# First loads in the order of their use, and the first contraction tile by halves, in a two-layer encoder trunk

## The chip, the cores and the metric

The kernel runs on one core of a Trainium2 chip. A core has a matrix engine (TensorE, "PE" in the profile, with its weight loads "PEld"), a vector engine (DVE), a scalar engine (ACT), GpSimd (POOL) and a queue engine (SP) from which this kernel starts all its transfers. The metric is the device time of one execution in microseconds (us); lower is better.

## The reference

Two layers of a bidirectional encoder over 256 positions and 1024 channels, in fp32. What is computed, cut to what matters here:

```
for i in range(2):
    h = rms_norm(x, norm_mix_pre[i])
    z = h @ w_in[i]                     # latents and rotary key, window q/k/v, three gates
    o_a = latent attention, 8 heads     # from the latents c_q, c_kv, k_rope
    o_b = Re(2-D DFT of h), 4 channel groups
    o_c = windowed attention (|t-s| <= 128) with a distance term and a sink, 8 heads
    merged = sigmoid(g_a)*(o_a @ w_branch_a) + sigmoid(g_b)*(o_b @ w_branch_b) + sigmoid(g_c)*(o_c @ w_branch_c)
    x = x + rms_norm(merged @ w_out)
    x = x + rms_norm(SwiGLU(rms_norm(x)))
    x = x + rms_norm((p[i] @ w_ple_proj) * sigmoid(x @ w_ple_gate))
```

## The kernel before

The activations lie with channels on the 128 partitions and the 256 positions along the row: `x` is eight tiles of 128 x 256, in the buffer `gx` behind the gains (columns `C_ALL`). A product with a 128 x 128 weight tile is one matmul of 256 columns. For fp32 accuracy each operand is split into a high part (the value rounded to the matmul type, written by ACT) and a low part (the rest, written by DVE), and each product takes three matmuls: high by high, high weight by low activation, low weight by high activation.

**Weights.** 279 chunks of eight weight tiles (512 KB) come from memory in the order of their use. Class `Weights` handles a chunk c in two steps: `load` (L146) starts the transfer into one of three staging buffers `w`; `split` (L160) writes `wh` on ACT (L175) and `wl` on DVE (L180) into one of three pairs of buffers, and then calls `load` for the chunk three places on. Chunk 0 is loaded and split in two halves of 512 columns (`pieces`, L156), every later one in one piece.

**Order.** PE, ACT and DVE run their instructions in the order in which this Python code calls them. That order is made by a planner, class `Order`: it keeps a clock `now`, which each planned matmul moves on by `T_MM` (0.109), and for each of ACT, DVE, POOL and the transfers the time at which it will be free (`free`). All side work is generators that yield the time at which they want to go on; whenever PE's code lets the clock move, the due ones are resumed and their instructions fall in between. Times that the planner believes decide only the order; what then waits on the chip is decided by semaphores. Buffers matter too: `take("f2", ...)` hands out one of six scratch buffers of 2 KB a partition, and a generator that finds none free yields until one is (L252). Among the users of `f2` are the angle tables (`posr`, `di`, `df`, `ang`, `nturn`), the latents (`c01`, `c23`, `zk`), the window's value and query (`zvs`, `zq0`), the Fourier tables (`dft`) and the squares of a norm.

**Start.** The opening loads x in five transfers with chunks 0, 1 and 2 between them, then the constants `cs` (identity and selector matrix, L435). While nothing is there to multiply, `keep_warm` puts small bf16 matmuls into PE's order (`warm`, L414; `WARM[0]` is their spacing by the planner's clock). `first_x` (L649) splits the eight tiles of x, `pre_norm` sums their squares, and `rstd` turns the sum into a row factor: PE sums over partitions (`ss_`), DVE scales (`ms_`), POOL raises to the power -1/2 (`rt_`, L497), PE spreads it over the partitions with the identity (`pr_`, L503), ACT copies it out (`R_`).

The first product is `k_outer` (L371): four pairs of output tiles, `z1` 0 to 3 (latents, rotary and window key, window value and first query), are accumulated side by side over the contraction tiles k = 0 to 5 of x. One k uses one chunk: eight weight tiles, 24 matmuls, in three passes over the four pairs: high weight with high x, low weight with high x, high weight with low x. The last two k (`LATE`) follow pair by pair in `mains` (L334), which runs over up to eight weight tiles of a chunk with both parts of the activation (L357, L358) and then with the low weights (L364).

`tables` (L669) asks for positions, sink and distance mask from the planner's time 6.0 on, has POOL form the differences of positions at 16.0, and from `TAB` = 18.0 on makes, by some dozen small DVE instructions, the distance (`dist`) and the rotary angles (`ang`, `nturn`), whose sine (`KC`) ACT takes. After the first product `latents` (L802) scales the four latent tiles, `window_vq0` (L856) the value and the first query, whose value is turned by PE (`vct`); `fourier_tables` splits the DFT tables; then the string `MIX` orders the pieces of the window attention, Fourier, gates (`gp`) and branches.

Of the kernel before, what the change touches and what calls it, by code (L numbers as in the profile page):

```python
# [17 lines left out]
P = 128  # L18
# [11 lines left out]


T_MM = 0.109
T_SEM = 0.18
MIX = "CCGGCCPPGPPGGBGGGBGGGBBG"
TAB = 18.0
PACE = 5.6
LATER = 0.3
ONACT = 2
STAGE = 3
WARM = (0.33, 0.15)  # L40
URGENT = (4.5, 2.5)
LATE = (2, 2, 2)
CT = 8
# [92 lines left out]
class Weights:  # L136
# [9 lines left out]
    def load(self):  # L146
        c, O = len(self.staged), self.O
        if c >= NCHUNK:
            return
        w = self.stage.tile([P, CT * P], F32, tag="w", name=f"w{c}")  # L150
        for s in self.pieces(c):
            self.nc.sync.dma_start(out=w[:, s], in_=self.dram[c, :, s])
        O.free["dma"] = max(O.free["dma"], O.now) + 1.5
        self.staged.append((w, O.free["dma"] + (2.0 if c else 1.0)))

    def pieces(self, c):  # L156
        n = CT * P // (1 if c else 2)
        return [slice(k, k + n) for k in range(0, CT * P, n)]

    def split(self):  # L160
# [23 lines left out]
    def idle(self, engine, c, us):  # L184

        O = self.O
        while (self.quiet or O.free[engine] > O.now + 0.1) and (c * CT - len(self.order)) * 3 * T_MM > us:
            yield O.now + 0.3
# [33 lines left out]
def encoder(ctx: ExitStack, tc: tile.TileContext, order, gxT, pT, pos, cst, dftT, mask, sink, wts, outT):  # L222
    nc = tc.nc
# [19 lines left out]
    O = Order()  # L243
    rd = {}
# [68 lines left out]
    ws = Weights(nc, O, stage, high, wts, order)  # L313

    def mm3(ps, lhs, rhs, start, stop, skip=False):
# [3 lines left out]
        T.matmul(ps, ll, rh, start=False, stop=stop, skip_group_check=skip)  # L319
        O.spend(3 * T_MM)  # L320

# [12 lines left out]
    def mains(ps, keys, rhs, start=True, stop=True, skip=False, there=None):  # L334

        i = 0
        while i < len(keys):
# [17 lines left out]
            for j in group:  # L355
                rh, rl = rhs(j)
                T.matmul(ps, w[j][0], rh, start=start and j == 0, stop=False, skip_group_check=skip)  # L357
                T.matmul(ps, w[j][0], rl, start=False, stop=False, skip_group_check=skip)  # L358
                O.spend(2 * T_MM)
                step()  # L360
# [10 lines left out]
    def k_outer(pairs, key, rhs, done, late):  # L371


        for k in range(KT - late):
            have(("x", k))
            if k == 0:
                weights(2 * len(pairs))
                keep_warm(None)
            weights(2 * len(pairs))
            w = [[ws.get(key(k, n, c)) for c in range(2)] for n in range(len(pairs))]  # L380
            xh, xl = rhs(k)
            for part, mov in ((0, xh), (1, xh), (0, xl)):
                for n in range(len(pairs)):
                    for c in range(2):
                        T.matmul(pairs[n][:, c, :], w[n][c][part], mov, start=(k == 0 and c == 0 and part == 0 and mov is xh),  # L385
                                 stop=False, skip_group_check=True)
                        O.spend(T_MM)
                    if n % 3 == 2:
                        O.step()
            ws.flush()  # L390
        for n in range(len(pairs)):
            ks = range(KT - late, KT)
            for c in range(2):
                mains(pairs[n][:, c, :], [key(k, n, c) for k in ks], lambda q: rhs(ks[q]), start=False, skip=True,
                      there=lambda q: ("x", ks[q]))
            done(n)
# [26 lines left out]
    mhalf = one.tile([P, 4], F32, tag="mhalf", name="mhalf")  # L423
    G.memset(mhalf, -0.5)
    S.activation(mhalf, mhalf, AF.Copy)
    O.free["dma"] = 0.75
    for j, n in ((0, 1), (1, 1), (2, 2), (4, 2), (6, 2)):
        s = slice(C_ALL + j * SEQ if j else 0, C_ALL + (j + n) * SEQ)
        nc.sync.dma_start(out=gx[:, s], in_=gxT[:, s])
        O.free["dma"] += 0.37 * n  # L430
        rd["x0", j] = rd["x0", j + n - 1] = O.free["dma"] + 1.5
        if j < 2 * STAGE - 1 and j != 1:
            ws.load()
    cs = one.tile([P, 2 * P], F32, tag="cs", name="cs")
    nc.sync.dma_start(out=cs, in_=cst)  # L435
    ident, sel = cs[:, :P], cs[:, P:]

    def gcol(i, name, j):
# [207 lines left out]
    st.XH, st.XL = xsplit_tiles("xs_first")  # L646
    ws.flush(3)

    def first_x():  # L649
        for j in range(KT):  # L650
            yield rd["x0", j]
            t = xhigh(st.XH, j, gcol(0, "norm_mix_pre", j))
            yield t
            rd["x", j] = xlow(st.XH, st.XL, j, gcol(0, "norm_mix_pre", j)) - 0.6
        O.start(pre_norm(st, "pre_first"), O.now)
# [12 lines left out]

    def tables():  # L669

        yield 6.0
        posr = yield from take("f2", "posr", (P, SEQ), I32)
        nc.sync.dma_start(out=posr, in_=pos.partition_broadcast(P))
        nc.sync.dma_start(out=posc, in_=pos.rearrange("(t p) -> p t", p=P))
        nc.sync.dma_start(out=snk, in_=sink.partition_broadcast(P))
        nc.sync.dma_start(out=dist, in_=mask)
        scale = (NOPE + ROPE) ** -0.5
        G.memset(TT, scale)
        yield 16.0
        di = yield from take("f2", "di", dt=I32)  # L680
        for q in range(2):
            G.tensor_tensor(out=di[:, q, :], in0=posr, in1=posc[:, q:q + 1].to_broadcast([P, SEQ]), op=ALU.subtract)
        O.run("pool", 1.5)
        yield TAB
        df = yield from take("f2", "df")
        yield from lazy()
        V.tensor_copy(df, di)
        drop(di, O.run("dve", 0.4))
        yield from lazy()
        stt(512, df, df, -1.0, df, ALU.mult, ALU.max)  # L690
        yield from lazy()
        rd["dist"] = tt(512, dist, dist, df, ALU.add)
        drop(df, rd["dist"])
        ang = yield from take("f2", "ang", (P, SEQ))
        n = yield from take("f2", "nturn", (P, SEQ))
        yield from lazy()
        V.tensor_copy(n, posr)
        drop(posr, O.run("dve", 0.2))
        yield from lazy()
        ts(256, ang, n, gs[:, C_COL:C_COL + 1], 0.0, ALU.mult, ALU.add)  # L700
        yield from lazy()
        ts(256, n, ang, 1.0 / (2 * math.pi), gs[:, C_COL + 3:C_COL + 4], ALU.mult, ALU.add)
        yield from lazy()
        ts(256, n, n, 12582912.0, -12582912.0, ALU.add, ALU.add)
        rest = 2 * math.pi
        for cpart in (6.28125, round((2 * math.pi - 6.28125) * 2 ** 21) / 2 ** 21, None):
            cpart = rest if cpart is None else cpart
            rest -= cpart
            yield from lazy()
            stt(256, ang, n, -cpart, ang, ALU.mult, ALU.add)  # L710
        yield from lazy()
        ts(256, ang, ang, gs[:, C_COL + 2:C_COL + 3], 3.1415925, ALU.add, ALU.min)
        t = ts(256, ang, ang, -3.1415925, gs[:, C_COL + 1:C_COL + 2], ALU.max, ALU.mult)
        drop(n, t)
        yield t
        t = act(256, KC, ang, AF.Sin)
        O.free["act"] += 1.3
        t += 1.3
        drop(ang, t)
        yield t  # L720
        yield from lazy()
        for own, r in ((1, slice(0, 64)), (0, slice(64, 128))):
            V.tensor_scalar_mul(TT[r, own, :], KC[r], scale)
            t = O.run("dve", 0.2)
        rd["tables"] = t
# [733 lines left out]
```

## Time and profile before

| | us |
|---|---|
| median of the runs (3; 918.1 to 919.2) | 918.32 |
| the profiled execution | 919.09 |
| its span in the profile | 917.2 |
| PE busy (7497 matmuls) | 897.5 |
| DVE busy (1066 instructions) | 690.5 |
| ACT busy (937 instructions) | 546.9 |

The span runs from the first to the last recorded instruction; the profiled execution took 1.9 us more than its span. A matmul is shown with its whole passage through the array, 0.28 us; in a row, one follows the other after 0.12 us. So two matmuls overlap, and a wait is best read from the start of one to the start of the next. On ACT and DVE an instruction begins some 0.1 us before the one ahead of it ends.

### The profile page before, as it was taken

To read this page: it belongs to the slowest core of one execution; us is meant where nothing else is said; L and a number is where in the kernel's file an instruction comes from. 1 tells how busy PE (TensorE), PEld (TensorE's weight loads), DVE (VectorE), ACT (ScalarE), POOL (GpSimd) and SP (SyncE) were. 2 spreads that over 40 slices of the span, in tenths; PEclk is the share of its full clock that TensorE was granted. 3 is DMA by queue.
4 is the path that set the end of the run, shared out by engine and by line. 5 is a ranking of instruction groups with operands and counts; after the bars stand their busy time and mean duration, and the time that the engine had idled before them with its cause. 6 is when DMAs were issued, how large, how long until landed. Compare 5 with 4: busy or idle time off the path is not lost.

```text
span 917.2 us, 18357 instructions
## 1 busy us (share of the span) xinstructions
PE 897.5 (98%) x7497; PEld 890.2 (97%) x7497; DVE 690.5 (75%) x1066; ACT 546.9 (60%) x937; POOL 34.5 (4%) x50
## 2 busy tenths in 40 slices
PE   8999999999999999999999999999999999999995
PEld 7999999999999999999999999999999999999995
DVE  6899888786887777445789998887858877764475
ACT  6688667645654445444657786776556545544444
POOL 2200000000000000000002000000000000000001
PEclk9999999999999999999999999999999999999998
DMA  7632544555556556554554344544655566555551
GB/s 255 188 123 82 172 160 139 165 173 182 169 168 211 185 185 185 184 184 138 171 156 145 105 138 133 178 157 146 199 178 171 179 190 188 187 174 177 184 163 69
DMA packets 43845, 152.25 MB, mean 166 GB/s; under 512 B 5232, under 2 KB 6000, under 8 KB 43760
## 3 DMA queue, kind: packets, MB, share of 16 engines
q1 hardware_dynamic: 43760, 151.07, 52.3%
q8 instruction: 59, 0.97, 0.4%
q14 instruction: 26, 0.21, 0.1%
HBM read 150.00 MB, written 1.05 MB: 165 GB/s over the span
## 4 chain that ended last, share of the span: by engine, by line
PE 90%; issue 4%; DVE 2%; POOL 2%; DMA 1%; ACT 0%; SPq 0%; DVEq 0%; POOLq 0%; ACTq 0%
PE ffL L364 8%; PE ffL L358 8%; PE ffL L357 8%; PE gpL L364 5%; PE ofL L364 5%; PE ofL L358 5%; PE ofL L357 5%; PE gpL L358 5%; PE gpL L357 5%; PE ffL L385 4%; PE brL L364 3%; PE brL L358 3%; PE brL L357 3%; PE z1L L385 2%; PE omL L364 2%
## 5 line engine op out<-in xcount | busy, mean ns | idle before, releaser
L180 DVE TENSOR_TENSOR wl<-w,wh 128x1024 fp32r<-128x1024 f32 (+1 forms) x280 | 339.9, 1218 | 92.1 <-ACT wh L175 91.5
L175 ACT ACTIVATE wh<-w 128x1024 fp32r<-128x1024 f32 (+1 forms) x280 | 293.8, 1054 | 192.8 <-PE ofL L358 49.6
L357 PE MATMUL ffL<-xs_mixL,wh 128*128 128x256 f32 x608 | 148.4, 281 | 0.0
L358 PE MATMUL ffL<-xs_mixL,wh 128*128 128x256 f32 x608 | 148.2, 281 | 0.0
L357 PEld LDWEIGHTS ffL<-xs_mixL,wh 128*128 128x128 f32 x608 | 114.7, 189 | 0.0
L358 PEld LDWEIGHTS ffL<-xs_mixL,wh 128*128 128x128 f32 x608 | 114.7, 189 | 0.0
L358 PE MATMUL ofL<-hidL,wh 128*128 128x256 f32 x352 | 87.0, 283 | 0.0
L357 PE MATMUL ofL<-hidH,wh 128*128 128x256 f32 x352 | 87.0, 283 | 0.0
L364 PE MATMUL ffL<-xs_mixL,wl 128*128 128x256 f32 x608 | 86.6, 281 | 0.0
L364 PEld LDWEIGHTS ffL<-xs_mixL,wl 128*128 128x128 f32 x608 | 78.3, 189 | 0.0
L358 PEld LDWEIGHTS ofL<-hidL,wh 128*128 128x128 f32 x352 | 67.0, 190 | 0.0
L357 PEld LDWEIGHTS ofL<-hidH,wh 128*128 128x128 f32 x352 | 67.0, 190 | 0.0
L357 PE MATMUL brL<-mixH,wh 128*128 128x256 f32 x256 | 64.1, 283 | 0.0
L358 PE MATMUL brL<-mixL,wh 128*128 128x256 f32 x256 | 64.0, 283 | 0.0
L285 DVE TENSOR_TENSOR fzL<-ffL,R_pre_mixL 128x512 f32<-128x512 f32 x44 | 30.0, 689 | 32.8 <-PE ffL L364 32.5
L364 PE MATMUL ofL<-hidH,wl 128*128 128x256 f32 x352 | 52.2, 284 | 0.0
L358 PEld LDWEIGHTS brL<-mixL,wh 128*128 128x128 f32 x256 | 49.0, 191 | 0.0
L357 PEld LDWEIGHTS brL<-mixH,wh 128*128 128x128 f32 x256 | 49.0, 191 | 0.0
L357 PE MATMUL gpL<-xs_pleL,wh 128*128 128x256 f32 x192 | 48.3, 284 | 0.0
L357 PE MATMUL gpL<-xs_first,wh 128*128 128x256 f32 x192 | 48.0, 283 | 0.0
L358 PE MATMUL gpL<-xs_pleL,wh 128*128 128x256 f32 x192 | 47.7, 281 | 0.0
L358 PE MATMUL gpL<-xs_first,wh 128*128 128x256 f32 x192 | 47.4, 280 | 0.0
(429 smaller groups left out, 2030.1 us busy)
## 6 DMA issues: line engine op xcount, KB each, us to landing
w<-wts SPq DMA_DIRECT2D x278, 512.0 KB, 3.5
dftL<-dft SPq DMA_DIRECT2D x6, 256.0 KB, 3.9
gx<-gx SPq DMA_DIRECT2D x3, 256.0 KB, 5.5
outT<-gx SPq DMA_DIRECT2D x3, 256.0 KB, 2.3
w<-wts SPq DMA_DIRECT2D x2, 256.0 KB, 3.3
p<-pT SPq DMA_DIRECT2D x2, 256.0 KB, 3.8
dist<-mask SPq DMA_DIRECT2D x1, 256.0 KB, 6.4
outT<-gx SPq DMA_DIRECT2D x2, 128.0 KB, 2.4
```

Source lines behind the costliest of these rows:

```text
L175: self.nc.scalar.activation(h[:, s], w[:, s], AF.Copy)
L180: self.nc.vector.tensor_tensor(out=l[:, s], in0=w[:, s], in1=h[:, s], op=ALU.subtract)
L285: V.tensor_tensor(out=out, in0=a, in1=b, op=op)
L357: T.matmul(ps, w[j][0], rh, start=start and j == 0, stop=False, skip_group_check=skip)
L358: T.matmul(ps, w[j][0], rl, start=False, stop=False, skip_group_check=skip)
L364: T.matmul(ps, w[j][1], rhs(j)[0], start=False, stop=stop and j == len(keys) - 1, skip_group_check=skip)
L385: T.matmul(pairs[n][:, c, :], w[n][c][part], mov, start=(k == 0 and c == 0 and part == 0 and mov is xh), stop=False, skip_group_check=True)
```

## The change

The transfers of the opening come in another order and in other sizes, the first contraction tile is multiplied in two halves, and the planner's figures for transfers are new (`T_DMA`: three numbers, of which one is used as KB per us). In the diff below, the first lines are the planner's; `pieces` now cuts chunks 0 and 1 into halves; `halves` in `k_outer` gives, for k = 0 alone, the three passes first for pairs 0 and 1 and then for pairs 2 and 3; `load_x` loads one tile each for x 0 to 3, with chunks 0, 1 and 2 between, and `later_x` loads tiles 4, 5 and 6, 7 at the planner's times 7.2 and 9.0; `cs` moves into `tables`, which begins at 11.0 instead of 6.0 and goes on at 19.0 and 21.0 instead of 16.0 and 18.0.

```
-TAB = 18.0
+T_DMA = (1.3, 310.0, 0.6)
+TAB = 21.0
-WARM = (0.33, 0.15)
+WARM = (0.37, 0.15)
...
-        O.free["dma"] = max(O.free["dma"], O.now) + 1.5
-        self.staged.append((w, O.free["dma"] + (2.0 if c else 1.0)))
+        O.free["dma"] = max(O.free["dma"], O.now + (T_DMA[0] if c >= STAGE else 0.0)) + 512 / T_DMA[1]
+        self.staged.append((w, O.free["dma"] + T_DMA[2] - (256 / T_DMA[1] if c < 2 else 0.0)))
     def pieces(self, c):
-        n = CT * P // (1 if c else 2)
+        n = CT * P // (1 if c > 1 else 2)
...
+        def halves(k, n, xh, xl):
+            three = ((0, xh), (1, xh), (0, xl))
+            if order and len(order) > 2 * n:
+                return [(range(n), *q) for q in three]
+            return [(ns, *q) for ns in (range(n // 2), range(n // 2, n)) for q in three]
...
-            for part, mov in ((0, xh), (1, xh), (0, xl)):
-                for n in range(len(pairs)):
+            for ns, part, mov in halves(k, len(pairs), xh, xl):
+                for n in ns:
...
-    for j, n in ((0, 1), (1, 1), (2, 2), (4, 2), (6, 2)):
+    def load_x(j, n):
         s = slice(C_ALL + j * SEQ if j else 0, C_ALL + (j + n) * SEQ)
         nc.sync.dma_start(out=gx[:, s], in_=gxT[:, s])
...
+    for j in range(3):
+        load_x(j, 1)
+        ws.load()
+    load_x(3, 1)
     cs = one.tile([P, 2 * P], F32, tag="cs", name="cs")
-    nc.sync.dma_start(out=cs, in_=cst)
...
+    def later_x():
+        for j, at in ((4, 7.2), (6, 9.0)):
+            yield at
+            load_x(j, 2)
...
-        yield 6.0
+        yield 11.0
+        nc.sync.dma_start(out=cs, in_=cst)
...
-        yield 16.0
+        yield 19.0
```

By this the queue of SP holds, in this order: x 0 (with the gains), chunk 0 in halves, x 1, chunk 1 in halves, x 2, chunk 2, x 3, chunk 3, chunk 4, x 4 and 5, x 6 and 7, chunk 5, `cs`, positions, sink, mask, chunk 6. Before, it held x 0, chunk 0 in halves, x 1, x 2 and 3, chunk 1, x 4 and 5, chunk 2, x 6 and 7, `cs`, chunk 3, positions, sink, mask, chunk 4.

Because every planned time after that moves, so does the order of the first layer on all engines, up to the feed-forward part. Three places of it follow.

On PE, the first contraction tile. Before, `wh_123` and `wl_124` are the high and low part of chunk 0 and each pass runs over all four pairs:

```order
L385 MATMUL z1L_0_136<-xs_first,wh_123 128x256 x2
L385 MATMUL z1L_1_137<-xs_first,wh_123 128x256 x2
L385 MATMUL z1L_2_138<-xs_first,wh_123 128x256 x2
L385 MATMUL z1L_3_139<-xs_first,wh_123 128x256 x2
L385 MATMUL z1L_0_136<-xs_first,wl_124 128x256 x2
L385 MATMUL z1L_1_137<-xs_first,wl_124 128x256 x2
L385 MATMUL z1L_2_138<-xs_first,wl_124 128x256 x2
L385 MATMUL z1L_3_139<-xs_first,wl_124 128x256 x2
```

Now (`wh_122`, `wl_123`) the twelve matmuls of pairs 0 and 1, which use the first half of the chunk alone, come ahead of those of pairs 2 and 3:

```order
L392 MATMUL z1L_0_135<-xs_first,wh_122 128x256 x2
L392 MATMUL z1L_1_136<-xs_first,wh_122 128x256 x2
L392 MATMUL z1L_0_135<-xs_first,wl_123 128x256 x2
L392 MATMUL z1L_1_136<-xs_first,wl_123 128x256 x2
L392 MATMUL z1L_0_135<-xs_first,wh_122 128x256 x2
L392 MATMUL z1L_1_136<-xs_first,wh_122 128x256 x2
L392 MATMUL z1L_2_137<-xs_first,wh_122 128x256 x2
L392 MATMUL z1L_3_138<-xs_first,wh_122 128x256 x2
L392 MATMUL z1L_2_137<-xs_first,wl_123 128x256 x2
L392 MATMUL z1L_3_138<-xs_first,wl_123 128x256 x2
```

The second half of the chunk is needed eight matmuls later than before.

On DVE, after the first product. Before, the angles are done by then, and the value `zvs` and first query `zq0` follow straight on the latents (`wl_490`, `wl_523` are chunks 10 and 11):

```order
L285 TENSOR_TENSOR c01L_476<-z1L_0_136,R_pre_first 128x512
L285 TENSOR_TENSOR c23L_477<-z1L_1_137,R_pre_first 128x512
L285 TENSOR_TENSOR zvsL_485<-z1L_3_139,R_pre_first 128x256
L289 SCALAR_TENSOR_TENSOR zq0L_504<-z1L_3_139,R_pre_first 128x256
L285 TENSOR_TENSOR zkL_478<-z1L_2_138,R_pre_first 128x512
L180 TENSOR_TENSOR wl_490<-w_423,wh_489 128x1024
L723 TENSOR_SCALAR TT<-KC 64x256 x2
L180 TENSOR_TENSOR wl_523<-w_446,wh_522 128x1024
```

Now most of the angles (`nturn`, `ang`) stand behind the latents (`ms_latL` and the scaled `c01`, `c23` belong to the latents' norm; `wl_521`, `wl_572` are chunks 11 and 12); `zvs` and `zq0` come after them:

```order
L286 TENSOR_TENSOR zkL_473<-z1L_2_137,R_pre_first 128x512
L294 TENSOR_SCALAR nturn<-ang,gx 128x256
...
L294 TENSOR_SCALAR ms_latL_550<-ss_latL_545 128x2 x2
L290 SCALAR_TENSOR_TENSOR ang<-nturn,ang 128x256
L294 TENSOR_SCALAR ang<-ang,gx 128x256 x2
L286 TENSOR_TENSOR mixL_134<-dftL_0_478,mixH_133 128x512
L181 TENSOR_TENSOR wl_521<-w_444,wh_520 128x1024
L181 TENSOR_TENSOR wl_572<-w_459,wh_571 128x1024
L290 SCALAR_TENSOR_TENSOR c01L_471<-c01L_471,gx,R_latL_586 128x256 x2
L290 SCALAR_TENSOR_TENSOR c23L_472<-c23L_472,gx,R_latL_586 128x256 x2
L286 TENSOR_TENSOR zvsL_589<-z1L_3_138,R_pre_first 128x256
L290 SCALAR_TENSOR_TENSOR zq0L_617<-z1L_3_138,R_pre_first 128x256
```

`zvs` has moved back by two chunks of weights and the latents' norm.

On DVE, further on, where the latent attention's queries (`qfa`, from PE's `qa`, with the tables `TT`) and keys (`kp`) begin. Before (`wl_1613` is chunk 28, `wl_1679`, `wl_1687` and `wl_1726` are 29 to 31, `saL` and `neg` belong to the first head):

```order
L285 TENSOR_TENSOR qfaL_0_1654<-qaL_0_1632,TT 128x512 [waits PE_49]
L180 TENSOR_TENSOR wl_1613<-w_1515,wh_1612 128x1024 [waits DMAHW2_49,Activation_49]
...
L1058 COPY kpL_0_1545<-mixL_135 64x256
L180 TENSOR_TENSOR wl_1679<-w_1557,wh_1678 128x1024 [waits DMAHW3_49,Activation_49]
L1076 TENSOR_REDUCE negaL0h_1737<-saL0h_1730 128x2 [waits PE_49]
L180 TENSOR_TENSOR wl_1687<-w_1616,wh_1686 128x1024 [waits DMAHW4_49,Activation_49]
L180 TENSOR_TENSOR wl_1726<-w_1657,wh_1725 128x1024 [waits DMAHW5_49,DVE_49,Activation_49]
L285 TENSOR_TENSOR qfaL_1_1785<-qaL_1_1633,TT 128x512 [waits PE_49]
```

Now (`wl_1660` is chunk 29):

```order
L286 TENSOR_TENSOR qfaL_0_1650<-qaL_0_1627,TT 128x512 [waits PE_49]
L181 TENSOR_TENSOR wl_1619<-w_1508,wh_1618 128x1024 [waits DMAHW4_49,Activation_49]
L286 TENSOR_TENSOR mixL_134<-oL0c_1603,mixH_133 128x256 [waits Activation_49]
L286 TENSOR_TENSOR qfaL_1_1702<-qaL_1_1628,TT 128x512 [waits PE_49]
L286 TENSOR_TENSOR mqL_1542<-qfaL_0_1650,mqL_1542 128x512 [waits Activation_49]
L181 TENSOR_TENSOR wl_1660<-w_1560,wh_1659 128x1024 [waits DMAHW5_49]
```

The low part of chunk 29 now stands behind `qfaL_1`, which waits for PE.

## Rows read from the trace of the kernel before

**Rows 1.** The page: the span and the busy time of each engine.
```profile
span 917.2 us, 18357 instructions
...
PE 897.5 (98%) x7497; PEld 890.2 (97%) x7497; DVE 690.5 (75%) x1066; ACT 546.9 (60%) x937; POOL 34.5 (4%) x50
```

**Rows 2.** Waits of PE: waiter, releaser, us in total, times, longest.
```profile
PE z1L L385 <- ACT wh L175: 1.5, 2, 0.8
...
PE pr_pre_first L503 <- POOL rt_pre_first L497: 0.8, 1, 0.8
...
PE ss_pre_first L486 <- DVE acc_npre_first L285: 0.3, 1, 0.3
```

**Rows 3.** Timeline, PE, opening: start, duration, instructions, [idle before <- releaser].
```profile
4.62 0.74 PE L385 MATMUL z1L<-xs_first,wh 128*128 128x256 f32 x4
6.16 0.74 PE L385 MATMUL z1L<-xs_first,wh 128*128 128x256 f32 x4 [0.79 <-ACT wh L175]
...
7.69 1.11 PE L385 MATMUL z1L<-xs_first,wh 128*128 128x256 f32 x8
9.54 1.22 PE L385 MATMUL z1L<-xs_first,wh 128*128 128x256 f32 x8 [0.74 <-ACT wh L175]
10.80 1.22 PE L385 MATMUL z1L<-xs_first,wl 128*128 128x256 f32 x8
```

**Rows 4.** Timeline, ACT, opening.
```profile
5.48 0.63 ACT L175 ACTIVATE wh<-w 128x512 fp32r<-128x512 f32 x1 [0.91 <-DMA w<-wts]
...
8.43 1.06 ACT L175 ACTIVATE wh<-w 128x1024 fp32r<-128x1024 f32 x1 [0.99 <-DMA w<-wts]
...
10.38 1.06 ACT L175 ACTIVATE wh<-w 128x1024 fp32r<-128x1024 f32 x1
```

**Rows 5.** Timeline, DVE, second half of chunk 0 and whole chunk 1.
```profile
6.14 0.69 DVE L180 TENSOR_TENSOR wl<-w,wh 128x512 fp32r<-128x512 f32 x1 [0.84 <-ACT wh L175]
...
9.52 1.23 DVE L180 TENSOR_TENSOR wl<-w,wh 128x1024 fp32r<-128x1024 f32 x1 [1.50 <-ACT wh L175]
```

**Rows 6.** Groups of POOL's line L497: duration ns min/median/max, first and last start.
```profile
L497 POOL TENSOR_TENSOR rt_mixL<-ms_mixL,mhalf x2: 695/696/697, 231.8 to 682.9; 128x2 f32<-128x2 f32 x2
```

**Rows 7.** Timeline, PE, DVE and POOL, around the first norm.
```profile
20.65 0.58 PE L486 MATMUL ss_pre_first<-ones,acc_npre_first 128*128 128x1 f32 x4 [0.32 <-DVE acc_npre_first L285]
...
22.16 0.15 DVE L293 TENSOR_SCALAR ms_pre_first<-ss_pre_first 128x2 f32<-128x2 f32 x1
...
22.45 2.48 POOL L497 TENSOR_TENSOR rt_pre_first<-ms_pre_first,mhalf 128x2 f32<-128x2 f32 x1 [6.34 <-DVE ms_pre_first L293]
...
23.03 1.22 DVE L180 TENSOR_TENSOR wl<-w,wh 128x1024 fp32r<-128x1024 f32 x1
```

**Rows 8.** Windows: length; PE, PEld, DVE, ACT, POOL busy; PE clock, DMA share, GB/s.
```profile
45.72:58.06 12.34, 12.34 (x105) 12.11 (x104) 12.07 (x25) 11.56 (x24) 1.06 (x4) 1.00 0.32 102
108.00:126.00 18.00, 17.88 (x151) 17.67 (x151) 13.65 (x22) 12.20 (x23) 0.00 (x0) 1.00 0.48 160
```

**Rows 9.** Timeline, DVE, up to and in the first of these windows.
```profile
43.94 1.41 DVE L285 TENSOR_TENSOR qcL<-zqL,qcL 64x512 fp32r<-64x512 f32 x2
...
45.72 0.68 DVE L289 SCALAR_TENSOR_TENSOR sbcL<-dist,scL 128x512 f32<-128x512 f32 x1
46.43 0.69 DVE L987 TENSOR_REDUCE mxcL<-sbcL 128x2 f32<-128x512 f32 x1
47.15 0.23 DVE L293 TENSOR_SCALAR negcL<-mxcL,snk 128x2 f32<-128x2 f32 x1
...
49.65 0.87 DVE L285 TENSOR_TENSOR qcL<-zqL,qcL 64x256 fp32r<-64x256 f32 x2
50.55 0.69 DVE L285 TENSOR_TENSOR mixL<-dftL,mixH 128x512 fp32r<-128x512 f32 x1
51.16 0.74 DVE L289 SCALAR_TENSOR_TENSOR UL<-puL,rt_pre_first,UL 128x512 fp32r<-128x512 f32 x1
...
56.93 1.21 DVE L180 TENSOR_TENSOR wl<-w,wh 128x1024 fp32r<-128x1024 f32 x1
```

More of the change, by code (lines that the diff above doesn't have):

```diff
@@ L425, in encoder @@
     S.activation(mhalf, mhalf, AF.Copy)
-    O.free["dma"] = 0.75
-    for j, n in ((0, 1), (1, 1), (2, 2), (4, 2), (6, 2)):
+    O.free["dma"] = 1.95
+    def load_x(j, n):
         s = slice(C_ALL + j * SEQ if j else 0, C_ALL + (j + n) * SEQ)
         nc.sync.dma_start(out=gx[:, s], in_=gxT[:, s])
[L430 to L433, printed above, removed]
+        O.free["dma"] = max(O.free["dma"], O.now + (T_DMA[0] if j > 3 else 0.0)) + ((s.stop - s.start) / 2) / T_DMA[1]
+        rd["x0", j] = rd["x0", j + n - 1] = O.free["dma"] + T_DMA[2]
+    for j in range(3):
+        load_x(j, 1)
+        ws.load()
+    load_x(3, 1)
     cs = one.tile([P, 2 * P], F32, tag="cs", name="cs")
-    nc.sync.dma_start(out=cs, in_=cst)
     ident, sel = cs[:, :P], cs[:, P:]
@@ L647, in encoder @@
     ws.flush(3)
+    def later_x():
+        for j, at in ((4, 7.2), (6, 9.0)):
+            yield at
+            load_x(j, 2)
+    O.start(later_x())
     def first_x():
         for j in range(KT):
+            while ("x0", j) not in rd:
+                yield O.now + 0.3
             yield rd["x0", j]
```

## The prediction

> **What bounds the kernel now.** First the page's busy times: PE works 897.5 of 917.2 us, DVE 690.5 [rows 1]. PE sets the end, so an edit counts only as far as it takes idle time from PE or gives it some. Next the list of PE's waits: in the part that the change touches they are the first product's on the high weights (1.5, twice), the first norm's row factor (0.8) and its sum (0.3) [rows 2]. Then the timeline of PE, ACT and DVE for the opening and for the first norm [rows 3 to 5, 7], to see what each wait ended on. Last the windows behind it: from 45.72 to 58.06 PE is busy all of the 12.34 us, DVE 12.07 of them; from 108 to 126 PE is busy 17.88 of 18.00 [rows 8]. The reader is to see two things. At most some 2.6 us of waiting can go. And behind the first product PE waits for nothing, though DVE runs level with it: there a shift of DVE's work has no slack.
>
> The unit of the sums is PE's pace, 105 matmuls in 12.34 us, 0.1175 us each [rows 8]. DVE's instructions are taken a little shorter than their duration, since each begins before the last one ends: the mixture 0.69 long starts its successor 0.61 later [rows 9], so 0.08 less.
>
> **The opening.** The first pass of k = 0 starts at 4.62; its four matmuls of pairs 0 and 1 end by 4.62 + 0.47 = 5.09, those of pairs 2 and 3 start at 6.16: 1.07 lost. The third pass of k = 0 starts at 7.69 and would be through at 8.63; k = 1 starts at 9.54: 0.91 lost. Its low pass starts at 10.80 where 9.54 + 0.94 = 10.48 would do: 0.32 lost [rows 3]. Together 2.3. Each ends on ACT's copy of a chunk, and that on a landing: second half of chunk 0 at 5.48, chunk 1 at 8.43 [rows 4]. Between these two landings 896 KB came (x 1, x 2 and 3, chunk 1) in 2.95 us, 304 KB per us.
>
> At that pace, from 5.48 on with the new sequence: x 1 (128 KB) and the first half of chunk 1 (256) land at 6.7, its second half at 7.6, x 2 at 8.0, chunk 2 at 9.7, chunk 3 behind x 3 at 11.8. PE, with 12 matmuls of pairs 0 and 1 first: the low weights of the first half, 0.69 long on DVE [rows 5], keep it some 0.2; the high ones of the second half are there at 5.48 + 0.63 = 6.11, before PE comes to them; the low ones end at 6.14 + 0.69 = 6.83, some 0.1 late. So k = 0 ends near 7.8 instead of 8.63. Chunk 1's first half is copied by 6.7 + 0.63 = 7.3 and its second by 8.2, needed at 7.8 and 8.0 or a little later, so k = 1 goes through to 10.6. Chunk 2 is copied whole by 9.7 + 1.06 = 10.8 and its low part takes 1.23 more [rows 5]: about 0.2 of wait. Behind it the loads are ahead. Left: 0.2 + 0.1 + 0.2 to 0.3, near 0.6; gained 2.3 − 0.6 = **1.7**. Bounds: 2.3 if all lands early, 0.8 if small transfers land slower and k = 1 stays as late as now. `cs` and the tables' inputs, later on the queue, are used only from the first norm on.
>
> **The first norm.** The sum's wait of 0.3 goes, as the squares are done when PE gets to it: **−0.3**. One warming matmul fewer (17, not 18) is in time that PE has anyway: 0. The row factor is another matter. Before, 24 matmuls stand between the sum and the spreading product, and the wait is still 0.84, part of it because DVE's scaling stood behind a chunk's low part and started at 22.16, 1.5 after the sum [rows 7]. Now only 10 matmuls stand between. The scaling can start about 0.6 after the sum, its end; from the scaling to the spreading product the trace has 24.99 − 22.16 = 2.8, nearly all of it POOL's power of 2.48 [rows 7]. So 3.4 from the sum, of which the sum's matmuls fill 0.44 and the ten 1.2: a wait of 1.75, **+0.9**. The power is what is uncertain: the same operation on the same two columns takes 0.70 elsewhere [rows 6]; then the wait is about 0 and the term −0.8. I take the 2.48, because it is this very instruction, and because the code before it on POOL stays the same.
>
> Why is it 2.48? From 23.03 to 24.25 DVE forms a low part, which reads two operands [rows 7]; 0.70 [rows 6] after that is 24.95, about the power's end, 22.45 + 2.48 = 24.93. That can be chance. The Trainium skill, page "SBUF — State Buffer", section "SBUF: two separate sides", says that GpSimd and VectorE share a pair of ports as an exclusive lock, and that a VectorE instruction with two SBUF inputs keeps out a GpSimd one that reads SBUF for its whole length. The trace fits that but does not show it. By the rule the power would now stand behind the difference's product, a low part and the `dist` sum, some 2.5 us from its start and then its own 0.7, and the term would be +1.6 instead of +0.9.
>
> **DVE after the first product.** Here is the cost that I expect to turn the sign. Angles and latents share the six scratch buffers. Begun three planner units later, the angles now stand behind the latents, and `zvs` and `zq0` stand behind two chunks and the latents' scaling. The turn of the value (`vct`) on PE follows them, the scaled queries on DVE wait for `vct`. So DVE waits for PE at about 43 us, and from there it has this to do until the low part of chunk 14: five additions or scalings of 512 columns (0.61 each [rows 9]: 3.0), two Fourier sums `U` (0.74 − 0.08: 1.3), two pairs `qc` of 256 columns (0.90 from start to start: 1.8), two single ones of 256 (0.45: 0.9), one pair `qc` of 512 (1.4), two heads' scores with maximum (0.71 + 0.72 + 0.15: 3.2), the low parts of chunks 13 and 14 (1.21 − 0.08: 2.3) [rows 9]. In all 13.9. PE has 102 matmuls from `vct` to the first that reads that low part: 12.0. It waits 1.9, or more if DVE is held at the scores, which PE also has to deliver. Against this, DVE may enter the stretch sooner than I reckon, as the opening is earlier. I take **+1.7**; bounds 0 and 2.3. Before, a stretch of the same length runs level (12.07 against 12.34 [rows 8]).
>
> **Chunk 29.** Its low part now stands behind `qfa` 1, which needs PE's last `qa`, and behind one more addition: 0.28 passage + 0.61 + 0.61 + 1.13 = 2.6 after that matmul, while PE has 13 matmuls (1.5) before it reads that part. **+1.1**; bounds 0 and 2.2 (one low part more ahead of it). Before, the low parts of chunks 29 to 31 stood ahead of `qfa` 1, and there PE hardly waits [rows 8].
>
> **Other visits.** Between the two places PE turns the window heads' probabilities, three times behind a chain on DVE whose place has moved. One low part in front of one of them would be 1.13, none 0: **+0.6**. The second layer and the feed-forward parts keep their order: 0. Four more small transfers cost SP only issue time.
>
> **Sum.** −1.7 − 0.3 + 0.9 + 1.7 + 1.1 + 0.6 = +2.3. The profiled execution, 919.09 (its span and 1.9 around it), would become 921.4; it lies 0.77 above the median of the runs, 918.32, so that the forecast is **920.6**, 0.25% slower. Two thousandths, 1.84 us, is about what can be told from no change.
>
> **Rivals.**
> 1. Faster: the opening gives its 1.7 and 0.3, and DVE is level again before chunk 14, since PE reaches `vct` later than DVE needs it only by some tenths. For it: DVE has 12.07 in 12.34, so a lead of 2 us is enough to hide all. Against it: the order puts `zvs` behind chunk 12's low part. Time: −2.0, with a short power −2.8: 915.5 to 916.3. Chance 0.22.
> 2. No change: the race before chunk 14 gives the opening back (−2.0 + 0.9 + 1.1 to 1.7) and chunk 29 is hidden, its low part being ready because PE waits earlier: 918.3 to 918.9. Together with the upper part of the first case and the lower of the forecast, chance 0.30.
> 3. Slower by more: the power held for as long as DVE's operands occupy the ports (+0.7 on the forecast; the page named above), the race at 2.3 (+0.6): 921.9. Or small loads that land no sooner, at the lower bound of the opening (+0.9): 921.5. It decides from the point where the spreading product waits over 2 us. Chance 0.13; 0.35 stay for the forecast.
>
> So slower has 0.48, faster 0.22, no change 0.30. The range goes from the upper end of the first case to somewhat above the third, 916.2 to 922.6; the forecast's own, 919.6 to 921.6.
>
> **What would show it.** In the changed kernel's profile: PE's first twelve matmuls without a gap over 0.3, k = 1 starting near 7.8, and no wait on ACT over 0.4 (opening). The spreading product waiting 1.7 with the power again about 2.5 long; 0.7 would give the first norm to the first rival. `vct` on PE near 43 us, a wait of PE on DVE's low part near 57 us, and another near 121; low parts (`wl`) among the releasers in PE's list of waits, where there are none before. If PE waits nowhere between 44 and 126 us, the forecast fails at the DVE terms and the kernel is faster; if the opening still waits over 1.5, it fails at the landing rate.

## The result, and the profile after

The changed kernel takes 924.07 us (median of 5 runs, 923.3 to 925.2), the one before 918.32: ratio 1.0063, 95% interval 1.005 to 1.0077. The sign is as forecast, the size more than twice as large, and the time lies outside the range of 916.2 to 922.6. The profiled execution took 923.3 us, of which 921.5 are the span; it is 4.2 longer than the profiled one of before (4.3 by the spans), while the medians differ by 5.75. The profiles below account for the 4.3; executions of one kernel differ by some 2 to 5 us, and the profiled one of before was a long one, that of after a short one.

The page of the changed kernel, as [rows 1]:

```profile
span 921.5 us, 18364 instructions
...
PE 899.2 (98%) x7496; PEld 889.9 (97%) x7496; DVE 691.7 (75%) x1067; ACT 548.0 (59%) x938; POOL 30.9 (3%) x50
```

PE's waits between 28 and 160 us (waiter, releaser, us in total, times, longest). The kernel before has one:

```profile
PE pr_latL L503 <- POOL rt_latL L497: 0.4, 1, 0.4
```

The changed kernel has these:

```profile
PE gpL L365 <- DVE wl L181: 2.1, 2, 1.5
PE gpL L358 <- DVE UL L290: 0.8, 1, 0.8
PE ptcL L948 <- DVE sbcL L942: 0.6, 1, 0.6
PE ptcL L948 <- ACT sbcL L282: 0.5, 1, 0.5
PE poL0c L972 <- ACT escL L282: 0.4, 1, 0.4
```

The opening on PE, as [rows 3], with the sum and the spreading of the first norm:

```profile
4.73 0.89 PE L392 MATMUL z1L<-xs_first,wh 128*128 128x256 f32 x4
...
7.54 2.04 PE L392 MATMUL z1L<-xs_first,wh 128*128 128x256 f32 x12
9.41 1.10 PE L392 MATMUL z1L<-xs_first,wl 128*128 128x256 f32 x8
...
17.28 1.20 PE L392 MATMUL z1L<-xs_first,wh 128*128 128x256 f32 x8 [0.16 <-ACT wh L176]
...
21.86 1.21 PE L392 MATMUL z1L<-xs_first,wl 128*128 128x256 f32 x8 [0.20 <-DVE wl L181]
...
24.82 0.58 PE L496 MATMUL ss_pre_first<-ones,acc_npre_first 128*128 128x1 f32 x4 [0.58 <-DVE acc_npre_first L286]
...
26.82 0.71 PE L513 MATMUL pr_pre_first<-cs,rt_pre_first 128*128 128x128 f32 x4
```

The low pass of k = 1 starts at 9.41, where it was 10.80: the gain of the opening is there. But k = 4 and 5 now wait a little, and the sum waits longer. Why, ACT shows: x 4 and 5 stand in the queue behind chunk 4 and are first read at 15.37.

```profile
15.37 0.91 ACT L282 ACTIVATE xs_first<-gx 128x256 fp32r<-128x256 f32 x2 [2.84 <-DMA gx<-gx]
```

The window behind it (length; busy time and instructions of PE, PEld, DVE, ACT, POOL; PE's clock, DMA share, GB/s), first of the changed kernel, then of the one before:

```profile
44.00:60.00 16.00, 13.68 (x113) 13.30 (x113) 14.68 (x27) 14.37 (x29) 1.15 (x4) 1.00 0.23 70
```
```profile
44.00:60.00 16.00, 16.00 (x136) 15.77 (x135) 15.63 (x30) 14.06 (x29) 1.06 (x4) 1.00 0.32 90
```

From 44 to 60 us PE does 113 matmuls instead of 136, and DVE, whose lateness stops it, is itself idle for 1.3, 0.9 of it in waits for PE. The DVE rows there show where it begins:

```profile
43.11 0.42 DVE L286 TENSOR_TENSOR zvsL<-z1L,R_pre_first 128x256 f32<-128x256 f32 x1
...
43.78 0.68 DVE L286 TENSOR_TENSOR mixL<-dftL,mixH 128x512 fp32r<-128x512 f32 x1
44.85 0.69 DVE L290 SCALAR_TENSOR_TENSOR zqL<-zq12L,R_pre_first 128x512 f32<-128x512 f32 x1 [0.39 <-PE vctL L886]
...
58.21 1.22 DVE L181 TENSOR_TENSOR wl<-w,wh 128x1024 fp32r<-128x1024 f32 x1
```

`zvs` comes at 43.11, PE's turn of the value (`vct`) at 44.43; DVE does the first query and one mixture meanwhile, and then stands 0.39 for it. Two waits of PE follow from the delay, on the Fourier sum `U` and on the low part of chunk 14, the row at 58.21:

```profile
46.34 0.36 PE L358 MATMUL gpL<-xs_first,wh 128*128 128x256 f32 x1 [0.81 <-DVE UL L290]
...
59.48 1.21 PE L365 MATMUL gpL<-xs_first,wl 128*128 128x256 f32 x8 [1.50 <-DVE wl L181]
```

To account for the 4.3 us of span I take the starts of PE's rows, one after the other, and count what each start lies behind the last one beyond the pace of 0.118. Summed by stage:

| stage | before | after | difference | forecast |
|---|---|---|---|---|
| opening, k = 0 to 3 | 2.1 | 0.6 | −1.5 | −1.7 |
| k = 4 and 5 | 0 | 0.9 | +0.9 | 0 |
| first norm, sum and spreading | 1.5 | 1.0 | −0.5 | +0.6 |
| latents' norm, to 44 us | 0.8 | 0.3 | −0.5 | 0 |
| 44 to 60 us | 0 | 2.65 | +2.65 | +1.7 |
| 60 to 110 us | 0.15 | 2.5 | +2.35 | +0.6 |
| 110 to 160 us | 0.3 | 1.45 | +1.15 | +1.1 |
| sum | 4.85 | 9.4 | +4.55 | +2.3 |

The sum comes to within 0.25 of the 4.3; this rest was not traced.

### The profile page after: what moved, and what is told of

Its sections match the earlier page's. It is cut to its first block, busy times and chain, and to the rows that moved or that the text cites. A ratio compares the mean times of both kernels' runs of the same rounds, so it can differ in the third digit from the quotient of the medians.

```text
span 921.5 us, 18364 instructions
## 1 busy us (share of the span) xinstructions
PE 899.2 (98%) x7496; PEld 889.9 (97%) x7496; DVE 691.7 (75%) x1067; ACT 548.0 (59%) x938; POOL 30.9 (3%) x50
## 3 DMA queue, kind: packets, MB, share of 16 engines
HBM read 150.00 MB, written 1.05 MB: 164 GB/s over the span
## 4 chain that ended last, share of the span: by engine, by line
PE 86%; DVE 5%; issue 4%; POOL 1%; DMA 1%; ACT 1%; SPq 0%; DVEq 0%; POOLq 0%; ACTq 0%
PE ffL L365 8%; PE ffL L358 8%; PE ffL L359 8%; PE ofL L365 5%; PE ofL L359 5%; PE ofL L358 5%; PE gpL L365 4%; PE gpL L358 4%; PE gpL L359 4%; PE ffL L392 4%; PE brL L365 3%; PE brL L359 3%; PE brL L358 3%; PE z1L L392 2%; PE omL L365 2%
```

## The experiments

Each is timed against runs of the kernel before on the same chip (its medians there: 917.4 to 918.4), so that kernels of different rows compare by their ratios.

| kernel | median | ratio to before, 95% interval |
|---|---|---|
| x1 loads alone, old order | 919.30 | 1.0014 (1.0005 to 1.0023) |
| x2 loads and halves, old order | 919.13 | 1.0011 (1.0000 to 1.0021) |
| x3 halves alone, old order | 918.05 | 0.9996 (0.9987 to 1.0005) |
| x4 changed, without halves | 923.72 | 1.0059 (1.0045 to 1.0073) |
| y1 changed, angles in own buffers | 919.27 | 1.0012 (1.0003 to 1.0020) |
| y2 changed, one angle buffer freed | 922.97 | 1.0059 (1.0045 to 1.0073) |
| y3 before, tables late | 925.39 | 1.0074 (1.0062 to 1.0086) |
| y4 changed, tables early | 925.73 | 1.0083 (1.0071 to 1.0096) |
| z1 mixed planner figures, own buffers | 918.51 | 1.0009 (0.9999 to 1.0019) |
| z2 y1 with x 4 to 7 sooner | 919.17 | 1.0021 (1.0012 to 1.0031) |
| z3 halves, scaling first | 917.68 | 0.9992 (0.9983 to 1.0002) |
| z4 z3 with constants later | 916.73 | 0.9991 (0.9982 to 1.0000) |

**Loads or order?** In x1 and x2 the loads are issued as in the change, but the planner keeps its old figures for them, so that the engines' order stays that of before. The core of the edit (x3 has the halves and `pieces` alone):

```
+    for j in range(3):
+        load_x(j, 1)
+        ws.load()
+    load_x(3, 1)
+    O.free["dma"] = 0.75
+    ... (rd and ws.staged get the planner's times of before)
```

> The kernel before with the changed order and sizes of the first loads alone: every engine's instructions stand as before (only chunk 1 is split in two pieces), no halves. Theory A (the loss is the planner's new order of the engines, the loads themselves are harmless): within 1.5 us of before, no wait of PE on DVE between 44 and 126 us. Theory B (the loads cost: x 4 to 7 land 5 us later, at 15 to 16 us, and small transfers land slower): 2 us or more slower, with the loss as waits on x or on chunks 3 to 6 before 25 us.

> The same with the first contraction tile by halves: loads and halves of the change, order of all engines otherwise that of before. Theory A: 0 to 2 us faster than before, as the opening's waits (2.3 us) shrink by about 1.6 and what is left is returned in part at the first norm; no wait on DVE between 44 and 126 us. Theory B: 2 us or more slower.

> The halves alone on the loads and the order of before (chunk 1 arrives and is split in halves, too). Both theories: the wait of 0.9 at 6.16 us goes, the one at 9.54 us is shorter; the first norm's wait of 0.8 on POOL grows by what the opening gains if the norm's chain is tied to the landing of x and not to PE. Time: within 1 us of before, or 1 to 1.5 us faster if the norm's chain follows PE.

> The changed kernel with the first contraction tile undivided; every other instruction as in the changed kernel. Both theories: 0.5 to 0.8 us more in the opening, so 0 to 0.8 us slower than the changed kernel (924.1), 0 where waits behind it swallow it.

x1 and x2 are 0.9 and 0.7 us slower than before by the medians (1.3 and 1.0 by the ratios), not 5.75: theory A, though x2 was expected up to 2 us faster and is not. In x2, loads and halves are there, and between 28 and 160 us PE has the one wait of before:

```profile
PE pr_latL L514 <- POOL rt_latL L508: 0.4, 1, 0.4
```

So the loss is the order of the engines, which only the planner's figures and times changed. What I had not expected is that the loads bring no gain in the old order, either: there ACT takes x 3 ahead of chunk 1, and as x 3 now stands behind chunk 2 in the queue, PE waits 3.18 us before k = 1 and then runs at a lower clock for a while (last section). ACT's rows of x2:

```profile
10.12 0.51 ACT L282 ACTIVATE xs_first<-gx 128x256 fp32r<-128x256 f32 x1 [1.13 <-DMA gx<-gx]
10.54 1.14 ACT L176 ACTIVATE wh<-w 128x512 fp32r<-128x512 f32 x2
```

The new loads need a new order of ACT, and with ACT's the planner changed all. The halves are worth nothing that can be told: 0.4 us in x3, and x4 without them is no slower than the change. Without them PE loses 0.5 more up to k = 3, but 0.7 less at k = 4 and 5, and waits 1.2 instead of 0.6 for the squares' sum, which begins at 24.87 instead of 24.82: what the halves gain is gone by then.

**Which part of the order?** The angles hold two of the six scratch buffers until they are done. y1 takes them out of there, y2 only one; y3 gives the kernel before the late tables; y4 gives the changed kernel the early ones.

```
-        ang = yield from take("f2", "ang", (P, SEQ))
-        n = yield from take("f2", "nturn", (P, SEQ))
+        ang = KC
+        n = yield from take("acc", "nturn", (P, SEQ))
```

(This is y1, where `drop(ang, t)` goes as well, since there is no buffer to hand back; y2: the change of `ang` alone; y3: 16 and 18 become 19 and 21; y4: the reverse.)

> The changed kernel with the angles out of the six scratch buffers: `ang` is formed in `KC` (its sine is taken in place), `nturn` in the buffer of the squares' sum, which is free by then. The tables keep their late times. In the order zvs and zq0 now follow straight on c01 and c23, as before the change. Theory S (the loss is the two buffers that the late angles hold, so that zvs and zq0 must wait for the latents): most of the waits of PE between 44 and 126 us go, 3 us or more faster than the changed kernel (924), 917 to 920. Theory L (late tables by themselves put some dozen DVE instructions, about 5 us, behind the first product, wherever they are kept): 922 or more.

> The changed kernel with `ang` alone formed in `KC`, so that the angles hold one scratch buffer and not two. Theory S: zvs or zq0 still has none in time, so the waits stay in the main: 921 to 924. Theory L: as the changed kernel, 922 to 925. (It tells whether one buffer is enough.)

> The kernel before with the tables' planned times alone moved (differences at 19, `TAB` 21, instead of 16 and 18); loads as before. Theory S: the angles hold the buffers when the latents want them, zvs falls behind a chunk of weights, and PE waits on DVE between 44 and 126 us: 921 to 924. Theory P (the planner's new figures for transfers and their shift of the whole order make the loss, not the tables): 918 to 919.

> The changed kernel with the tables' times of before (differences at 16, `TAB` 18). By the planner's clock the latents come earlier too, and in its order zvs still stands behind the chunk after the latents. Theory S: still slow, 921 to 925. Theory L: back at 918 to 920, since the angles' work starts as early as before.

y1 came out in theory S's range and outside L's; y2 lies in both ranges, so that it only tells that one buffer is not enough. y3 and y4 rule out S's rivals (918 to 919 and 918 to 920), but lie 1.4 and 0.7 us above S's own ranges. y3 is the strongest: two planner times alone, with the loads of before, cost 0.74%. It is more than the whole change, and as far as its one profile tells that is the clock: PE runs slower for a while behind two of its waits, some 2.6 us in all, and in y4 behind one, some 1.4 (last section). PE's waits of y3 from 28 to 200 us:

```profile
PE gpL L364 <- DVE wl L180: 2.1, 2, 1.9
PE puL L318 <- DVE mixL L285: 1.2, 1, 1.2
PE pr_latL L503 <- POOL rt_latL L497: 1.1, 1, 1.1
```

And y1 gets back most: 1.0063 becomes 1.0012. In its DVE rows the value and first query again stand right behind the latents. But the angles' work has moved, too: in the change its last step starts at 38.38, in y1 four steps come between 61 and 67 us:

```profile
31.62 0.68 DVE L286 TENSOR_TENSOR c23L<-z1L,R_pre_first 128x512 f32<-128x512 f32 x1
32.22 0.41 DVE L286 TENSOR_TENSOR zvsL<-z1L,R_pre_first 128x256 f32<-128x256 f32 x1
32.55 0.41 DVE L290 SCALAR_TENSOR_TENSOR zq0L<-z1L,R_pre_first 128x256 f32<-128x256 f32 x1
...
61.16 0.42 DVE L290 SCALAR_TENSOR_TENSOR KC<-nturn,KC 128x256 f32<-128x256 f32 x1
...
66.24 0.73 DVE L294 TENSOR_SCALAR KC<-KC,gx 128x256 f32<-128x256 f32 x2
```

`zvs` at 32.22 instead of 43.11. PE's waits from 28 to 160 us there:

```profile
PE ptcL L947 <- ACT sbcL L282: 0.8, 2, 0.5
PE pabL L318 <- DVE UL L290: 0.6, 1, 0.6
PE gpL L365 <- DVE wl L181: 0.2, 1, 0.2
```

They are 1.6 where the change has 4.4. Counted by the starts, as in the table, y1 loses 0.3 from 44 to 60 us (the change 2.65) and 0.3 from 110 to 160 us (1.45), but still 2.3 from 60 to 110 us (2.5): 0.7 at 60.8, 65.8 and 88.3 each and 0.2 at 77.7. So the two buffers account for the losses at chunk 14 and chunk 29, and not for those in between. Nor does y1 part the buffers from the place of the angles' work, which moved with them.

y4 refutes the view that early tables cure it: with the opening planned shorter, the latents come early as well and still meet the angles. Its first product even waits 2.1 on a low part, as DVE stands 3.0 us for the difference of positions, which POOL can only form at 19.53, when they have landed.

**A version that beats both?**

> A version meant to beat both: the loads and halves of the change, x 4 to 7 where the change has them, the planner's old figures for transfers with the later times of x 2 to 7 alone put in, the angles out of the scratch buffers (`ang` in `KC`, `nturn` in the buffer of the squares' sum), differences at 20 and `TAB` 22. Theory S: zvs and zq0 straight on c01 and c23, few waits between 44 and 126 us (about 2 us in all), the opening and first norm 1.5 us shorter than before: 916.5 to 918.5, against 918.3 before. If the planner's other shifts of the order cost as well (as in the kernel with its own buffers for the angles): 918.5 to 920.

> The changed kernel with the angles out of the scratch buffers, as in the earlier run, and x 4 to 7 asked for at the planner's 5.0 and 6.0 instead of 7.2 and 9.0, so that they stand one chunk earlier in the queue. If the late landing of x 4 to 7 (15 to 16 us) makes the waits on chunks 4 and 5 and on the squares' sum (1.7 us in all between 17 and 25 us): these go to 0.9 or less, 0.7 us faster than the earlier run (918.6 against 919.3). If DVE's load makes them: no change in these waits.

z1 undoes nearly all (918.51, at the border of its two forecasts) and does not beat before; from 60 to 110 us it loses 2.4 by the starts, hardly less than the change. In z2 the waits at k = 4 and 5 are gone, but the squares' sum waits 1.2, where y1 and the change have 0.6, so that the three together come to 1.2 and not to the 0.9 or less that was expected:

```profile
PE ss_pre_first L496 <- DVE acc_npre_first L286: 1.2, 1, 1.2
```

Against its own chip's before z2 is no faster than y1 (1.0021 and 1.0012). So most of what k = 4 and 5 give is taken back by the wait for the squares; the rest can't be followed, as z2's order is another further on (from 110 to 160 us PE loses 2.1 there by the starts, in y1 0.3). z3 and z4 shorten the first norm's chain in the order of before:

```
+        while c in (5,) and not getattr(self, "go", False):
+            yield O.now + 0.05
...
+        ws.go = True
...
+        yield 10.0
+        nc.sync.dma_start(out=cs, in_=cst)
```

(The first lines hold chunk 5's low part until the norm's scaling is issued; the last two are z4's; PE's spreading product keeps its place by 1.6 of planner time.)

> A version meant to beat both: the kernel before with halves of chunks 0 and 1 and of the first contraction tile, and in the first norm DVE's scaling ahead of chunk 5's low part (it stood behind it and began 1.5 us after the sum); all else in the order of before. Theory N (the opening's gain is returned at the first norm, whose chain is tied to the landing of x and to DVE, not to PE): with the chain 1.1 us shorter the wait on POOL falls from 1.0 to 0.2 or less, and 0.8 to 1.5 us come out: 916.5 to 917.3 where before is 917.6 to 918.4. If the power on POOL takes longer in its new neighbourhood (2.5 us before beside a chunk's low part), no gain.

> The last version with one part of the change more: the constants (`cs`, positions, sink, mask) are asked for behind chunk 4, at the planner's 10, instead of around chunk 3; x as before. In the last version chunk 5 landed at 17.8 us behind them and PE waited 1.1 at 19 us. If the loads make that wait, chunk 5 lands near 15.5 to 16.5, the wait goes, and 0.7 to 1.2 us come out beside the last version: 916.2 to 917.2, clearly under before (917.6 to 918.4). If the first norm's chain (squares, sum, power) takes it back: as the last version, 917.7. From 44 us on all as before.

In z3 the spreading product no longer waits, but PE stands 1.07 before the high weights of the chunk that lands at 17.8 (it is chunk 4; the text on z4 calls it 5). z3 is 0.75 faster than before by the medians, just under the 0.8 to 1.5 that theory N gave it, and its interval holds 1. In z4 the wait at chunk 4 is gone, too, and the span of its profile is 914.3, 2.9 shorter than that of before; but the medians give 0.7 (0.9991, up to 1.0000). z4 has the lowest median, at the edge of what can be told from before, and by the ratios it is where z3 is: the 0.7 to 1.2 expected beside z3 did not come.

## Why the prediction was wrong

The direction held, and so did the mechanism at chunk 14 and chunk 29: the opening gives, and DVE's work behind the first product takes more. The size was off. By the table the stages miss the forecast by +0.2, +0.9, −1.1, −0.5, +0.95, +1.75 and +0.05, 2.25 in all; the two norms, 1.6 better than forecast, hid part of the miss, and that was luck.

- **The opening: right, with a part missing.** 1.7 forecast, 1.5 measured for k = 0 to 3. I let the loads be "ahead" from there; but x 4 and 5 stand behind chunk 4, and that waits for chunk 1's split. 0.9 came back at k = 4 and 5.
- **The first norm: wrong sign.** Forecast +0.6, measured −0.5. By the starts the sum's wait, which I had let go, grew from 0.5 to 0.7, and the spreading product's fell from 1.0 to 0.3. The power took 1.03, not 2.48, and DVE's scaling was on time. The rival with the power held longer falls:

```profile
25.74 1.03 POOL L507 TENSOR_TENSOR rt_pre_first<-ms_pre_first,mhalf 128x2 f32<-128x2 f32 x1 [5.62 <-DVE ms_pre_first L294]
```
```profile
25.51 0.68 DVE L290 SCALAR_TENSOR_TENSOR df<-df 128x512 f32<-128x512 f32 x1
26.11 1.22 DVE L181 TENSOR_TENSOR wl<-w,wh 128x1024 fp32r<-128x1024 f32 x1
```

  The power began while `df` ran, which reads two operands (the same tile twice) until 26.19, and ended at 26.77, 0.58 later. The forecast took the 2.48 of before, and the rival had the power kept out by three such instructions in a row; it came in behind the first. By the Trainium skill, page "SBUF — State Buffer", section "SBUF: two separate sides", a VectorE (DVE) instruction with two SBUF inputs that has begun keeps such a power out for its whole length, and a power that has begun keeps the VectorE instruction out. The trace agrees with the first; the second it does not bear out: the low part begins at 26.11, before the power ends, and takes its usual 1.22. I had also set only 0.70 against the 2.48. The same operation takes 1.62 at 254.57 us in the kernel before, where a low part runs as it begins.
- **DVE after the first product: right mechanism, term too small.** `vct` at 44.43 (forecast near 43), PE's wait on chunk 14's low part at 59.48 with 1.5 (forecast 1.7 to 1.9 near 57). I had not seen the wait on `U` before it, 0.8, which DVE's `zq`, late itself, holds up. y1, with the two buffers freed, loses 0.3 in this stretch; y3, with the old loads and the buffers held, 2.1.
- **Chunk 29: right.** PE waits 0.64 for its low part at 124.67 (with chunk 14's 1.5 this is the 2.1 of the list of waits); by the starts 0.8, forecast 1.1.
- **Other visits: the step that failed.** "+0.6", with one low part as the upper bound. Measured from 60 to 110 us: +2.35, and at the two largest waits no low part stands in the chain. They are the softmax chains of window heads (0.8 at 72, 0.9 at 88, 0.2 at 101, 0.5 at 106 us). The one at 72: scores to maximum on DVE, exponentials on ACT, sums and scaling on DVE, turn on PE, with 41 matmuls (4.8 us) on PE between scores and turn:

```profile
66.58 0.69 DVE L290 SCALAR_TENSOR_TENSOR sbcL<-dist,scL 128x512 f32<-128x512 f32 x1 [0.88 <-PE scL L1001]
```
```profile
69.54 0.42 ACT L282 ACTIVATE obL<-asbL 1x256 f32<-1x256 f32 x1 [1.86 <-DVE obL L286]
69.86 0.49 ACT L282 ACTIVATE sbcL<-sbcL,negcL 128x256 f32<-128x256 f32 x1
```
```profile
72.06 0.72 PE L948 MATMUL ptcL<-cs,sbcL 128*128 128x128 f32 x4 [0.63 <-DVE sbcL L942]
```

  The exponentials stand behind `ob` on ACT, a copy of one row, which waits 1.86 for DVE; from the scores' row to the exponentials are 3.3 us. Before, nothing stood between:

```profile
63.38 0.69 DVE L289 SCALAR_TENSOR_TENSOR sbcL<-dist,scL 128x512 f32<-128x512 f32 x1 [0.58 <-PE scL L981]
```
```profile
65.14 0.51 ACT L281 ACTIVATE sbcL<-sbcL,negcL 128x256 f32<-128x256 f32 x1
```

  There it is 1.8. At 88 an `ob` that waits 1.56 stands ahead of the exponentials, too, but the turn waits for the scaling, which here is ACT's. It could begin at 85.14 and stands behind a chunk's high part and three copies:

```profile
84.91 1.04 ACT L176 ACTIVATE wh<-w 128x1024 fp32r<-128x1024 f32 x1
...
87.27 0.89 ACT L282 ACTIVATE sbcL<-sbcL,invcL 128x256 f32<-128x256 f32 x2
```

  Before, this scaling began at 87.13, no sooner; but there PE came to the turn only at 88.77, here at 87.82. So the larger part of the term lies in the places of ACT's and PE's work, not in one low part on DVE, and I had bounded it by the wrong thing. What moves these places is open: with the two buffers freed (y1) 2.3 of the 2.5 are still lost in this stretch, though at other points.
- **From profile to median.** I took the median 0.77 under the profiled execution; of the changed kernel it lies 0.8 above. With the measured 4.2 and that offset the time would have been 922.5, barely inside the range; the other 1.5 lies in which execution was profiled.

## What to carry to other kernels

Where a planner's clock sets the order, correcting its figures in one place re-deals everything behind it; look for the resource that flips (here two scratch buffers held by late, unhurried work) and give that work buffers of its own. Keep the physical change and the change of order apart in an experiment: issue the new loads with the old figures. And before a wait at the start is worth taking away, ask what the stage's end hangs on: here the wait for the squares' sum took back what the halves gave (x4) and most of what the sooner x gave (z2).

## What the hardware showed

How long POOL's power takes goes with the DVE instruction that is under way when it begins. In the first norm of the 14 profiles here it took 0.72 and 0.76 where none with two operands in SBUF was (z4, y3), 1.58 where a low part was (z3), and 1.03 to 1.05 in the eight where `df` or `dist` was. In these nine it ended 0.57 to 0.58 after that instruction, as in z3 (22.30 + 1.23 = 23.53, and 24.10):

```profile
22.52 1.58 POOL L501 TENSOR_TENSOR rt_pre_first<-ms_pre_first,mhalf 128x2 f32<-128x2 f32 x1 [5.24 <-DVE ms_pre_first L295]
```
```profile
22.30 1.23 DVE L182 TENSOR_TENSOR wl<-w,wh 128x1024 fp32r<-128x1024 f32 x1
```

In the other three (before, x1, x3) it began during `dist`, too, but took 2.48 and ended only 0.69 after the low part that follows. The order of instructions does not decide between the two: x1 and x2 have the same DVE instructions around it (`ms`, `dist`, cast, low part), starting within 0.03 us of each other:

```profile
24.00 2.48 POOL L506 TENSOR_TENSOR rt_pre_first<-ms_pre_first,mhalf 128x2 f32<-128x2 f32 x1 [4.91 <-DVE ms_pre_first L294]
```
```profile
23.98 1.05 POOL L508 TENSOR_TENSOR rt_pre_first<-ms_pre_first,mhalf 128x2 f32<-128x2 f32 x1 [5.37 <-DVE ms_pre_first L294]
```
```profile
23.76 0.69 DVE L286 TENSOR_TENSOR dist<-dist,df 128x512 f32<-128x512 f32 x1
```

The last row is of x2. What decides whether the power comes in behind `dist` or only behind the low part is open. It is one candidate for part of the 2 to 5 us by which executions of one kernel differ; that was not tested.

In x2, after PE had stood 3.18 us, its granted clock fell: 24 matmuls instead of 34 in the 4 us from 12 on, at 0.61, that is partly at 1.2 and partly at 2.4 GHz.

```profile
11.21 1.74 PE L388 MATMUL z1L<-xs_first,wh 128*128 128x256 f32 x8 [3.18 <-ACT wh L176]
```
```profile
8.00:12.00 4.00, 0.82 (x6) 0.80 (x6) 1.78 (x4) 2.06 (x4) 0.00 (x0) 0.96 1.03 383
12.00:16.00 4.00, 4.00 (x24) 4.00 (x24) 3.42 (x7) 3.93 (x8) 0.00 (x0) 0.61 0.55 163
```

y3 shows the same 0.61 after a wait of 1.57 at 10.05. Further on the clock fell behind waits of 1.9 on a low part: in y2 at 58.35 (0.66 from 60 to 64 us), in y3 at 126.58 (0.72 from 126 to 130) and in y4 at 126.59 (0.62). It stayed at 1.00 after x1's wait of 2.1 at 11.07, y4's of 2.1 at 22.96 and the change's 1.5 at 59.48, so that the length of the wait alone does not tell. Such a wait can cost more than itself: 10 matmuls, 1.2 us, in x2 and in y3's opening, and 12, 1.4 us, further on in y3 and y4 (51 matmuls from 126.58 to 134 us where 63 fit).
